# A recurrence's post-processing cut into six pieces, and the first interactions of each half recorded later

## The chip, the cores and the metric

The kernel runs on one core of one Trainium2 chip, with its five engines: TensorE (PE, matmuls), VectorE (DVE), ScalarE (ACT), GpSimd (POOL) and SyncE (SP, which issues DMAs). The metric is the device time of one execution in microseconds (us), lower is better. Each engine works off its own list of instructions in order; semaphores tie the lists together.

## The reference

An encoder trunk of two layers over 1024 tokens of width 1024, in fp32. Layer 0 mixes by a gated MLP and pooling, layer 1 by RWKV-7; a SwiGLU feed-forward network follows each, and a final RMS norm. The part that matters here is layer 1's mixer:

```python
def step(state, inp):                       # per token, 16 heads of 64
    r_t, w_t, k_t, v_t, a_t, b_t = inp
    sa = jnp.einsum('bhvk,bhk->bhv', state, a_t)
    state = (state * w_t[:, :, None, :] + sa[..., None] * b_t[:, :, None, :]
             + v_t[..., None] * k_t[:, :, None, :])
    return state, jnp.einsum('bhvk,bhk->bhv', state, r_t)
...
mean = jnp.mean(y, axis=-1, keepdims=True)
var = jnp.mean(jnp.square(y - mean), axis=-1, keepdims=True)
y = ((y - mean) * lax.rsqrt(var + GN_EPS)).reshape(bsz, seq, d)
y = y * ln_w.astype(f32) + ln_b.astype(f32)
bonus = jnp.sum(rh * kh * r_k.astype(f32), axis=-1, keepdims=True) * vh
y = (y + bonus.reshape(bsz, seq, d)).astype(h.dtype)
return (y * g) @ w_o, v_first
```

The state passes from token to token; the lines behind it, a norm over each head, its weight and bias, a bonus and a gate, are the post-processing that the change moves.

## The kernel before

The 1024 tokens are worked in two halves of 512, h = 0 and 1. A dense product in fp32 is three matmuls of split operands (high by high, low by high, high by low: lines 405 to 407); a weight tile of 512 KB is loaded by ACT's DMA queue into one of three raw buffers (`raw`), converted to its high part by ACT (L157: `whi`, `wdhi`) and to its low part by DVE (L158: `wlo`, `wdlo`).

The recurrence of a half (`recur`) goes through eight chunks, c = 0 to 7, of 64 tokens, 16 heads at a time. It runs beside the dense products of a feed-forward network: `drive` records both, step by step, at a ratio of 6.2 (half 0) or 3.0 (half 1), the steps of the recurrence with a higher priority. The number that a step yields says how much dense work is recorded before the next. The framework's scheduler then fixes each engine's list from these priorities and its own model of time; the kernel has no list of its own for this stretch.

The names of a chunk's work, in its order:

- `load(c)`: SP's DMAs of the chunk's operands (`ar`, `bk`, `uv`, `xx`).
- `gram(c, q)`, q = 0, 1: "first interactions", 32 matmuls `sm<-ar,bk` into two PSUM buffers, masked on DVE into `gt` (L1530).
- `flip_bk`: eight transposes `sm<-ident,bk` into two PSUM buffers, copied by ACT (L1541).
- `below`, `below2`: the inverse of the chunk's triangular part; `below2` ends with two copies into `XT` (ACT L1570, DVE L1571).
- `own`: `sm<-uv,gt` and `sm<-S,ar`, joined in `Q` (ACT L1582, DVE L1583).
- `ou`/`yp`: `sm<-Q,XT` and `yp<-S,ar`; `ou` is copied into `uv` (ACT L1605, DVE L1606).
- the state: `sm<-uv,bkt`, then two DVE operations (L1616, L1617) into the next `S`.
- `yp<-uv,gt` completes the output, copied into `ysb` (ACT L1629).

`burst(c)` records these for chunk c, with gram(c+1, 0) between own and ou, gram(c+1, 1) between ou and the state, and then flip_bk(c+1), load(c+2) and below(c+1). In this stretch PSUM has 3 buffers for dense products (`mm`), 4 for the recurrence (`sm`, used in turn) and one for `yp`.

After each odd chunk, `post` normalises the outputs of two chunks: DMAs of `gch` and `vch`, the bonus on POOL (L1668), 16 `bn_stats` on DVE (L1672), six small DVE operations for mean and variance (L1676 to L1681), the power −1/2 on POOL (`rsqrt`, L410), the mean's factor (L1683), the second chunk scaled on ACT (L1687, eight instructions), the first on DVE (L1690, L1691), and for each of the two a multiplication by the weight and the addition of `vch` (L1694, L1695). It is recorded as a whole between that chunk's burst and the next one's, in the middle of the dense work there, with three yields of 0.3. Then `turn_out`, called inside the next burst behind flip_bk, transposes the result on PE (`sm<-ident,ysb`, eight), gates it (L1711, eight on DVE) and stores it to `y_d`, from which the output projection reads it back.

Of the kernel before, what the change touches and what calls it, by code (L numbers as in the profile page):

```python
# [32 lines left out]
BESIDE = 2  # L33

# [9 lines left out]
def tile_trunk(  # L44
# [358 lines left out]

    def mm3(o, whi, wlo, xhi, xlo, first, last):
        pe.matmul(o, whi, xhi, start=first, stop=False)  # L405
        pe.matmul(o, whi, xlo, start=False, stop=False)  # L406
        pe.matmul(o, wlo, xhi, start=False, stop=last)  # L407
# [1053 lines left out]
    def recur(h, wp, stream):  # L1461
# [56 lines left out]
        def gram(c, q):  # L1518
            ar, bk, _, gt, _, _ = C[c]
            og = [pst("sm").rearrange("p (a b) -> p a b", b=P) for _ in range(2)]  # L1520
            for j in range(4):
                p = q * 4 + j
                for b in range(2):
                    for r in (1, 0):
                        mm(
                            og[r][rows[b], j, :], bk[rows[r], p, b, :],
                            ar[rows[r], p].rearrange("p a b -> p (a b)"), start=True, stop=True,
                        )
            for r in range(2):
                dve.tensor_tensor(  # L1530
                    out=gt[:, q * 4 : q * 4 + 4, r, :], in0=og[r], in1=bc(gm.unsqueeze(1), [P, 4, P]), op=ALU.mult
                )
# [27 lines left out]
        def below2(c, w1):  # L1560
            XT = C[c][5]
            ox = smt()
            for p in range(8):
                for r in (1, 0):
                    b0 = r * 64
                    mm(
                        ox[b0 : b0 + 32, p, 0:32], w1[b0 + 32 : b0 + 64, p, :], XT[b0 + 32 : b0 + 64, p, 32:64],
                        start=True, stop=True, tile_position=(b0 + 32, b0),
                    )
            act.activation(XT[0:32, :, 32:64], ox[0:32, :, 0:32], AF.Copy)  # L1570
            dve.tensor_copy(XT[64:96, :, 32:64], ox[64:96, :, 0:32])  # L1571

        def own(c, S0):
# [9 lines left out]
            dve.tensor_tensor(out=Q, in0=Q, in1=oq, op=ALU.add)  # L1583
            return Q

        def burst(c, bkt, w1):
# [3 lines left out]
            below2(c, w1)  # L1590
            Q = own(c, S0)
            yield 0.1
            if more:
                gram(c + 1, 0)
                yield 0.1
# [10 lines left out]
            dve.tensor_copy(uv[rows[1], 1], ou[rows[1]])  # L1606
            yield 0.1
            if more:
                gram(c + 1, 1)
                yield 0.1  # L1610
            if cg < NCH - 1:
# [5 lines left out]
                dve.tensor_tensor(out=Sn, in0=tS, in1=bc(pct[:, cg, :].unsqueeze(2), [P, 8, 64]), op=ALU.mult)  # L1617
                S[0] = Sn
                if c == 7:
# [13 lines left out]
            if more:  # L1633
                bkt = flip_bk(c + 1)
                if turned:
                    turned.pop()()
# [15 lines left out]
        turned = []  # L1652

        def post(jj):
# [14 lines left out]
            st = wt("st", 1, [P, 2, 8, 6])  # L1669
            for r in range(2):  # L1670
                for p in range(8):
                    dve.bn_stats(out=st[:, r, p, :], in_=ysb[r][:, p, :])  # L1672
            sts = st.rearrange("p a b s -> p (a b) s")
# [8 lines left out]
            rsqrt(var)  # L1682
            dve.scalar_tensor_tensor(out=mean, in0=mean, scalar=-0.5, in1=var, op0=ALU.mult, op1=ALU.mult)  # L1683
            yield 0.3
# [7 lines left out]
            yield 0.3  # L1692
# [3 lines left out]
            yield 0.3  # L1696
# [28 lines left out]
        yield 0.2  # L1725
# [7 lines left out]
        for c in range(8):  # L1733
            bkt, w1 = yield from burst(c, bkt, w1)
            yield BURST / 2
            if c % 2 == 1:
                yield from post(c // 2)
            yield BURST / 2
        turned.pop()()
# [225 lines left out]
    drive(ffn(0, 1, nxt["hn"], f, D0P[:3], nd=2), recur(0, wp, in_pieces(hb_pool, 1, h_d[1, 0])), 6.2)  # L1965
# [67 lines left out]
    drive(until(dense_a, flag), recur(1, wp, in_pieces(hp, 0, h_d[0, 1])), RATIO)  # L2033
# [44 lines left out]
```

## Time and profile before

| | us |
|---|---|
| median of three runs | 2395.51 |
| lowest, highest run | 2394.72, 2399.97 |
| the profiled execution | 2406.34 |
| its span | 2404.6 |
| PE busy in the span | 2324.9 |
| half 0's recurrence, about | 1042 to 1243 |
| half 1's recurrence, about | 1593 to 1810 |

The profile is one execution. A row of a timeline gives the start and the duration in us, the engine, the line of the kernel, what is written and read, and in brackets how long the engine had been idle and which operation released it. A row of waits gives the total, the number and the longest of such idle times. A row of windows gives a stretch and its length, each engine's busy time and instructions, and at its end PE's granted clock (1.00 is full), the DMA engines' busy share and GB/s.

### The profile page before, as it was taken

Reading aid. Unit: us, or ns where it says so; the run is one execution under the profiler, and the core shown is the slowest. Engines: PE = TensorE matmul, PEld = TensorE weight load, DVE = VectorE, ACT = ScalarE, POOL = GpSimd, SP = SyncE. Lnnn points to the kernel's source line nnn. Section 1 sums busy time; section 2 is a strip of 40 time slices with the busy share of each in tenths; the row PEclk is TensorE's granted clock in tenths of the full one; section 3 lists DMA queues with packets and bytes.
Section 4 is the critical chain, followed back from the end, with each engine's and each line's share of the span. In section 5 each row is a group of like instructions: output and inputs, shape, how many; then the busy total and the mean of one; then the engine's idle time right before and its main releaser. Section 6 shows DMA issues by size and latency. Waiting matters only on the chain.

```text
span 2404.6 us, 37640 instructions
## 1 busy us (share of the span) xinstructions
PE 2324.9 (97%) x15315; PEld 1903.6 (79%) x15315; DVE 1468.1 (61%) x2312; ACT 946.1 (39%) x1427; POOL 180.0 (7%) x226
## 2 busy tenths in 40 slices
PE   8999999999999999989999899999999999999998
PEld 6888888888788788777877678777778788888886
DVE  6445775665568858756768858756654446444443
ACT  6233444343224755423336555433332225222223
POOL 0200000000000022101100122101100001000001
PEclk9999999999999999999999999999999999999999
DMA  5114452334765565774545465676524333433231
GB/s 181 53 51 145 148 165 86 125 98 151 279 224 191 164 165 140 218 208 138 145 140 150 156 179 150 198 216 175 145 80 152 120 87 118 127 96 97 79 114 45
DMA packets 408333, 342.73 MB, mean 143 GB/s; under 512 B 79392, under 2 KB 352928, under 8 KB 407392
## 3 DMA queue, kind: packets, MB, share of 16 engines
q10 hardware_dynamic: 266048, 195.33, 27.4%
q1 hardware_dynamic: 142112, 145.01, 19.4%
q8 instruction: 120, 1.97, 0.3%
q14 instruction: 53, 0.43, 0.1%
HBM read 263.33 MB, written 76.94 MB: 142 GB/s over the span
## 4 chain that ended last, share of the span: by engine, by line
PE 75%; DVE 9%; DMA 7%; ACT 3%; issue 3%; POOL 2%; SPq 1%; ACTq 0%; POOLq 0%; DVEq 0%
PE mm L405 17%; PE mm L406 16%; PE mm L407 16%; PE mm L736 5%; PE mm L738 5%; PE mm L737 5%; PE sm L1483 4%; DVE wlo L158 1%; DMA raw<-in_ffn_w_down_dram 1%; DVE it L1435 1%; ACT whi L157 1%; DMA bk<-bk_d 1%; DVE xi L1440 1%; DMA raw<-y_d 1%; PE yp L1483 1%
## 5 line engine op out<-in xcount | busy, mean ns | idle before, releaser
L405 PE MATMUL mm<-ahi,whi 128*128 128x512 f32 x1376 | 541.7, 395 | 6.9 <-ACT ahi L157 4.9
L406 PE MATMUL mm<-alo,whi 128*128 128x512 f32 x1376 | 542.0, 394 | 3.0 <-DVE alo L158 3.0
L407 PE MATMUL mm<-ahi,wlo 128*128 128x512 f32 x1376 | 540.9, 394 | 1.0 <-DVE wlo L158 0.9
L157 ACT ACTIVATE whi<-raw 128x1024 fp32r<-128x1024 f32 (+2 forms) x284 | 286.1, 1014 | 491.8 <-PE mm L406 383.4
L158 DVE TENSOR_TENSOR wlo<-raw,whi 128x1024 fp32r<-128x1024 f32 (+2 forms) x284 | 337.4, 1192 | 220.4 <-ACT whi L157 193.6
L405 PEld LDWEIGHTS mm<-ahi,whi 128*128 128x128 f32 x1376 | 259.2, 188 | 65.3 <-ACT ahi L157 6.1
L406 PEld LDWEIGHTS mm<-alo,whi 128*128 128x128 f32 x1376 | 259.6, 189 | 60.4 <-DVE alo L158 4.3
L407 PEld LDWEIGHTS mm<-ahi,wlo 128*128 128x128 f32 x1376 | 259.5, 189 | 58.4 <-DVE wlo L158 2.3
L499 DVE TENSOR_TENSOR h<-h,mm 128x512 f32<-128x512 f32 x276 | 186.1, 684 | 160.2 <-PE mm L407 149.0
L405 PE MATMUL mm<-hidhi,wdhi 128*128 128x512 f32 x304 | 117.9, 394 | 2.8 <-ACT sg L953 2.8
L407 PE MATMUL mm<-hidhi,wdlo 128*128 128x512 f32 x304 | 119.0, 392 | 0.0
L406 PE MATMUL mm<-hidlo,wdhi 128*128 128x512 f32 x304 | 118.9, 392 | 0.0
L736 PE MATMUL mm<-ahi,whi 128*128 128x512 f32 x296 | 115.6, 390 | 0.0
L737 PE MATMUL mm<-alo,whi 128*128 128x512 f32 x296 | 115.2, 389 | 0.0
L738 PE MATMUL mm<-ahi,wlo 128*128 128x512 f32 x296 | 113.6, 389 | 0.0
L157 ACT ACTIVATE wdhi<-raw 128x1024 fp32r<-128x1024 f32 x42 | 43.5, 1057 | 166.7 <-PE mm L406 122.2
L961 DVE TENSOR_TENSOR sg<-sg,mm 128x512 f32<-128x512 f32 x52 | 35.7, 686 | 116.6 <-PE mm L407 116.6
L158 DVE TENSOR_TENSOR wdlo<-raw,wdhi 128x1024 fp32r<-128x1024 f32 x42 | 53.2, 1266 | 28.9 <-ACT wdhi L157 28.9
L405 PEld LDWEIGHTS mm<-hidhi,wdhi 128*128 128x128 f32 x304 | 57.5, 189 | 15.4 <-ACT sg L953 3.2
L407 PEld LDWEIGHTS mm<-hidhi,wdlo 128*128 128x128 f32 x304 | 57.4, 189 | 12.3 <-issue 0.3
L406 PEld LDWEIGHTS mm<-hidlo,wdhi 128*128 128x128 f32 x304 | 57.5, 189 | 11.8 <-issue 0.2
L405 PE MATMUL mm<-xhi,whi 128*128 128x512 f32 (+1 forms) x160 | 65.4, 409 | 0.0
(394 smaller groups left out, 4243.4 us busy)
## 6 DMA issues: line engine op xcount, KB each, us to landing
raw<-in_ffn_w_down_dram ACTq DMA_DIRECT2D x88, 512.0 KB
raw<-in_ffn_w_gate_dram ACTq DMA_DIRECT2D x74, 512.0 KB
raw<-in_ffn_w_up_dram ACTq DMA_DIRECT2D x74, 512.0 KB
hid_d<-hid SPq DMA_DIRECT2D x36, 512.0 KB
hd<-hid_d SPq DMA_DIRECT2D x26, 512.0 KB
raw<-in_ab_w_in_dram ACTq DMA_DIRECT2D x16, 512.0 KB
raw<-in_ab_w_out_dram ACTq DMA_DIRECT2D x16, 512.0 KB
raw<-in_rwkv_w_r_dram ACTq DMA_DIRECT2D x16, 512.0 KB
```

The source lines that it names most:

```text
L157: act.activation(hi, src, AF.Copy)
L158: (eng or dve).tensor_tensor(out=lo, in0=src, in1=hi.bitcast(F32), op=ALU.subtract)
L405: pe.matmul(o, whi, xhi, start=first, stop=False)
L406: pe.matmul(o, whi, xlo, start=False, stop=False)
L407: pe.matmul(o, wlo, xhi, start=False, stop=last)
L499: dve.tensor_tensor(out=H[h][:, m, :], in0=H[h][:, m, :], in1=o, op=ALU.add)
L736: pe.matmul(o, wh[:, k, :], x[0][:, k, :], start=st, stop=False, skip_group_check=True)
L737: pe.matmul(o, wh[:, k, :], x[1][:, k, :], start=False, stop=False, skip_group_check=True)
L738: pe.matmul(o, wl[:, k, :], x[0][:, k, :], start=False, stop=k == 3, skip_group_check=True)
L961: dve.tensor_tensor(out=s, in0=s, in1=o, op=ALU.mult)
L1435: dve.tensor_tensor(out=t, in0=bc(iat[:, j, j + 1 : 32].unsqueeze(2), sh), in1=bc(xi[:, j, 0 : j + 1].unsqueeze(1), sh), op=ALU.mult,)
L1483: i = f(*args, **kw)
```

## The change

`post` becomes a generator of six pieces and is no longer recorded in one go between two bursts. Its first step (the DMAs and the bonus) is taken after the odd chunk as before. The pieces are taken inside the next chunk's burst by `between()`, each recorded so that it stands behind the last DVE instruction of the chain step before it (`chain[0]`): the first chunk's bn_stats behind XT, the second's behind Q, mean to power behind gt, the scaling behind uv, and the two weight-and-`vch` pairs behind the second gt and the state. So the bn_stats of the even chunk, which stood behind that chunk's own burst, now stand two bursts later with the rest. After chunk 7 the remaining pieces are recorded with yields of 0.3.

`START` is the other edit: the first gram of a half is recorded behind two more dense products, and its first matmul is ordered behind the newest dense matmul.

```diff
--- before.py
+++ after.py
@@ -31,6 +31,8 @@
 BESIDE = 2
+
+START = 2
 
@@ -401,10 +403,12 @@
     def hsl(h):
         return slice(h * HT, (h + 1) * HT)
 
+    newest = [None]
+
     def mm3(o, whi, wlo, xhi, xlo, first, last):
         pe.matmul(o, whi, xhi, start=first, stop=False)
         pe.matmul(o, whi, xlo, start=False, stop=False)
-        pe.matmul(o, wlo, xhi, start=False, stop=last)
+        newest[0] = pe.matmul(o, wlo, xhi, start=False, stop=last).ins
 
     def rsqrt(t):
         pool.tensor_tensor(out=t, in0=t, in1=mhalf[:, : t.shape[1]], op=ALU.pow)
@@ -1458,7 +1462,7 @@
             )
     state_d = dram.tile([P, 8, 64], F32, name="state_d")
 
-    def recur(h, wp, stream):
+    def recur(h, wp, stream, ratio):
 
 
 
@@ -1527,9 +1531,9 @@
                             ar[rows[r], p].rearrange("p a b -> p (a b)"), start=True, stop=True,
                         )
             for r in range(2):
-                dve.tensor_tensor(
+                chain[0] = dve.tensor_tensor(
                     out=gt[:, q * 4 : q * 4 + 4, r, :], in0=og[r], in1=bc(gm.unsqueeze(1), [P, 4, P]), op=ALU.mult
-                )
+                ).ins
 
         def flip_bk(c):
             bk = C[c][1]
@@ -1568,7 +1572,7 @@
                         start=True, stop=True, tile_position=(b0 + 32, b0),
                     )
             act.activation(XT[0:32, :, 32:64], ox[0:32, :, 0:32], AF.Copy)
-            dve.tensor_copy(XT[64:96, :, 32:64], ox[64:96, :, 0:32])
+            chain[0] = dve.tensor_copy(XT[64:96, :, 32:64], ox[64:96, :, 0:32]).ins
 
         def own(c, S0):
 
@@ -1580,7 +1584,7 @@
                     mm(oq[rows[r], p, :], ar[rows[r], p, 0, :], S0[rows[r], p, :], start=True, stop=True)
             Q = wt("Q", 1, [P, 8, 64])
             act.activation(Q, ov, AF.Copy)
-            dve.tensor_tensor(out=Q, in0=Q, in1=oq, op=ALU.add)
+            chain[0] = dve.tensor_tensor(out=Q, in0=Q, in1=oq, op=ALU.add).ins
             return Q
 
         def burst(c, bkt, w1):
@@ -1588,10 +1592,13 @@
             ar, _, uv, gt, _, XT = C[c]
             cg, S0, more = h * 8 + c, S[0], c < 7
             below2(c, w1)
+            between()
             Q = own(c, S0)
+            between()
             yield 0.1
             if more:
                 gram(c + 1, 0)
+                between()
                 yield 0.1
             ou = smt()
             yp = psum["pool"].tile([P, 8, 64], F32, tag="y", bufs=1, name="yp")
@@ -1603,10 +1610,12 @@
                         skip_group_check=True,
                     )
             act.activation(uv[rows[0], 0], ou[rows[0]], AF.Copy)
-            dve.tensor_copy(uv[rows[1], 1], ou[rows[1]])
+            chain[0] = dve.tensor_copy(uv[rows[1], 1], ou[rows[1]]).ins
+            between()
             yield 0.1
             if more:
                 gram(c + 1, 1)
+                between()
                 yield 0.1
             if cg < NCH - 1:
                 Sn = wt("S", 2, [P, 8, 64])
@@ -1614,8 +1623,10 @@
                 each(os_, lambda r, p: bkt[:, p, r * 64 : r * 64 + 64], lambda r, p: uv[:, r, p, :])
                 tS = wt("Q", 1, [P, 8, 64])
                 dve.tensor_tensor(out=tS, in0=S0, in1=os_, op=ALU.add)
-                dve.tensor_tensor(out=Sn, in0=tS, in1=bc(pct[:, cg, :].unsqueeze(2), [P, 8, 64]), op=ALU.mult)
+                chain[0] = dve.tensor_tensor(out=Sn, in0=tS, in1=bc(pct[:, cg, :].unsqueeze(2), [P, 8, 64]), op=ALU.mult)
+                chain[0] = chain[0].ins
                 S[0] = Sn
+                between()
                 if c == 7:
                     sp.dma_start(state_d, Sn)
                 yield 0.1
@@ -1632,7 +1643,9 @@
             yield 0.1
             if more:
                 bkt = flip_bk(c + 1)
-                if turned:
+                if turned or pieces:
+                    for _ in pieces.pop():
+                        pass
                     turned.pop()()
                 if c < 6:
                     load(c + 2)
@@ -1649,7 +1662,12 @@
                 yield 0.1
             return bkt, w1
 
-        turned = []
+        turned, chain, pieces = [], [None], []
+
+        def between():
+            if pieces:
+                with tc.issue_after(chain[0]):
+                    next(pieces[0], None)
 
         def post(jj):
             ysb = [ypair.pop(0) for _ in range(2)]
@@ -1667,9 +1685,11 @@
             b16 = bon[:, 2 * j : 2 * j + 2, :].rearrange("t c p -> t (c p)")
             pool.tensor_tensor(out=v16, in0=v16, in1=bc(b16.unsqueeze(2), [P, 16, 64]), op=ALU.mult)
             st = wt("st", 1, [P, 2, 8, 6])
+            yield
             for r in range(2):
                 for p in range(8):
                     dve.bn_stats(out=st[:, r, p, :], in_=ysb[r][:, p, :])
+                yield
             sts = st.rearrange("p a b s -> p (a b) s")
             mean, dm, var = (wt(n, 1, [P, 16]) for n in ("mean", "dm", "var"))
             me, mo, ve, vo = (sts[:, :, i] for i in (1, 4, 2, 5))
@@ -1680,8 +1700,8 @@
             dve.tensor_tensor(out=var, in0=var, in1=dm, op=ALU.add)
             dve.tensor_scalar(out=var, in0=var, scalar1=1.0 / 64, scalar2=GN_EPS, op0=ALU.mult, op1=ALU.add)
             rsqrt(var)
+            yield
             dve.scalar_tensor_tensor(out=mean, in0=mean, scalar=-0.5, in1=var, op0=ALU.mult, op1=ALU.mult)
-            yield 0.3
             vb, mb = (bc(t[:, 0:8].unsqueeze(2), [P, 8, 64]) for t in (var, mean))
             for p in range(8):
                 act.activation(
@@ -1689,11 +1709,12 @@
                 )
             dve.tensor_tensor(out=ysb[0], in0=ysb[0], in1=vb, op=ALU.mult)
             dve.tensor_tensor(out=ysb[0], in0=ysb[0], in1=mb, op=ALU.add)
-            yield 0.3
+            yield
             for q in range(2):
                 dve.tensor_tensor(out=ysb[q], in0=ysb[q], in1=lnw, op=ALU.mult)
                 dve.tensor_tensor(out=ysb[q], in0=ysb[q], in1=vch[:, q], op=ALU.add)
-            yield 0.3
+                if q == 0:
+                    yield
 
             def turn_out():
                 for q in range(2):
@@ -1722,7 +1743,8 @@
             stream_loaded = stream()
         with tc.issue_after(stream_loaded):
             load(1)
-        yield 0.2
+        yield START * ratio
+        last.append(newest[0])
         gram(0, 0)
         yield 0.5
         gram(0, 1)
@@ -1734,8 +1756,11 @@
             bkt, w1 = yield from burst(c, bkt, w1)
             yield BURST / 2
             if c % 2 == 1:
-                yield from post(c // 2)
+                pieces[:] = [post(c // 2)]
+                next(pieces[0])
             yield BURST / 2
+        for _ in pieces[0]:
+            yield 0.3
         turned.pop()()
         yield 1.0
 
@@ -1962,7 +1987,7 @@
     between = []
     prime_b, steps_b = down_steps(1, D0B[1], lambda f: whl(), hslot, True, spill_h, (next(between[0]) for _ in range(4)))
     prime_b()
-    drive(ffn(0, 1, nxt["hn"], f, D0P[:3], nd=2), recur(0, wp, in_pieces(hb_pool, 1, h_d[1, 0])), 6.2)
+    drive(ffn(0, 1, nxt["hn"], f, D0P[:3], nd=2), recur(0, wp, in_pieces(hb_pool, 1, h_d[1, 0]), 6.2), 6.2)
     wp_es.close()
     y, y_es = open_pool(name="y0", bufs=1, side="left")
     ys = open_act(("y", 0), y)
@@ -2030,7 +2055,7 @@
         1, 0, hnA, f, TAIL, last=True, between=y_pieces(), early=True,
         then={G1A[1][-1][-1]: lambda: flag.append(1), G1A[2][0][-1]: out_b},
     )
-    drive(until(dense_a, flag), recur(1, wp, in_pieces(hp, 0, h_d[0, 1])), RATIO)
+    drive(until(dense_a, flag), recur(1, wp, in_pieces(hp, 0, h_d[0, 1]), RATIO), RATIO)
     wp_es.close()
     ps_es.close()
     ps_es = open_psum("psd2", DENSE)
```

What this does to the lists, at the places that the prediction speaks of. (In the new kernel the same operations have line numbers that are 2 to 21 higher.)

DVE, half 0, the burst of chunk 4, before: from the copy into XT to the masks of gram(5, 1).

```order
L1571 COPY XT<-sm 32x8x32
L1690 TENSOR_TENSOR ysb<-ysb,var 128x512
L1683 SCALAR_TENSOR_TENSOR mean<-mean,var 128x16
L1691 TENSOR_TENSOR ysb<-ysb,mean 128x512
L1583 TENSOR_TENSOR Q<-Q,sm 128x512
L1694 TENSOR_TENSOR ysb<-ysb,lnw 128x512
L1695 TENSOR_TENSOR ysb<-ysb,vch 128x512
L1694 TENSOR_TENSOR ysb<-ysb,lnw 128x512
L1695 TENSOR_TENSOR ysb<-ysb,vch 128x512
L1530 TENSOR_TENSOR gt<-sm,gm 128x4x128 x2
L1606 COPY uv<-sm 64x512
L1530 TENSOR_TENSOR gt<-sm,gm 128x4x128 x2
```

The same place after, in two parts, first from XT to the second gt of gram(5, 0):

```order
L1575 COPY XT<-sm 32x8x32
L1691 BN_STATS st<-ysb 128x6 x8
L1587 TENSOR_TENSOR Q<-Q,sm 128x512
L1691 BN_STATS st<-ysb 128x6 x8
L1534 TENSOR_TENSOR gt<-sm,gm 128x4x128
L1696 TENSOR_TENSOR mean<-st 128x16
L1534 TENSOR_TENSOR gt<-sm,gm 128x4x128
```

and from the last small operation ahead of the power to the state's two operations:

```order
L1701 TENSOR_SCALAR var<-var 128x16
L1613 COPY uv<-sm 64x512
L1704 SCALAR_TENSOR_TENSOR mean<-mean,var 128x16
L1710 TENSOR_TENSOR ysb<-ysb,var 128x512
L1711 TENSOR_TENSOR ysb<-ysb,mean 128x512
L1534 TENSOR_TENSOR gt<-sm,gm 128x4x128
L1714 TENSOR_TENSOR ysb<-ysb,lnw 128x512
L1534 TENSOR_TENSOR gt<-sm,gm 128x4x128
L1715 TENSOR_TENSOR ysb<-ysb,vch 128x512
L1625 TENSOR_TENSOR Q<-S,sm 128x512
L1626 TENSOR_TENSOR S<-Q,pct 128x512
```

The 16 bn_stats and the small rows now stand between XT and uv, and the mean row, which takes the power's result from POOL, with two wide `ysb` rows stands between uv and the second pair of gt.

PE, the same burst, from gram(5, 1) on. Before:

```order
L1483 MATMUL sm<-ar,bk 64x128 x16
L1483 MATMUL sm<-uv,bkt 64x64 x16
L1483 MATMUL yp<-uv,gt 64x64 x16
L1483 MATMUL sm<-ident,bk 128x128 x8
L1483 MATMUL sm<-ident,ysb 128x128 x8
L405 MATMUL mm<-ahi,whi 128x512
L406 MATMUL mm<-alo,whi 128x512
```

After:

```order
L1487 MATMUL sm<-ar,bk 64x128 x16
L1487 MATMUL sm<-uv,bkt 64x64 x16
L1487 MATMUL yp<-uv,gt 64x64 x16
L1487 MATMUL sm<-ident,bk 128x128 x8
L1487 MATMUL sm<-ident,ysb 128x128
L410 MATMUL mm<-alo,whi 128x512
L411 MATMUL mm<-ahi,wlo 128x512
```

The first transpose of `ysb` still follows the flips directly; the other seven stand behind 11 dense matmuls. Further up in the same burst (rows not shown), 18 dense matmuls stood inside gram(5, 0) before; now 4 stand between gram(5, 0) and ou.

PE, half 0, the first gram, before:

```order
L405 MATMUL mm<-hidhi,whi 128x512
L406 MATMUL mm<-hidlo,whi 128x512
L407 MATMUL mm<-hidhi,wlo 128x512
L406 MATMUL mm<-hidlo,whi 128x512
L407 MATMUL mm<-hidhi,wlo 128x512
L1485 MATMUL sm<-ar,bk 64x128
L1483 MATMUL sm<-ar,bk 64x128 x31
L405 MATMUL mm<-hidhi,whi 128x512
```

After:

```order
L409 MATMUL mm<-hidhi,whi 128x512
L410 MATMUL mm<-hidlo,whi 128x512
L411 MATMUL mm<-hidhi,wlo 128x512
L410 MATMUL mm<-hidlo,whi 128x512
L411 MATMUL mm<-hidhi,wlo 128x512
L1487 MATMUL sm<-ar,bk 64x128 x32
L409 MATMUL mm<-hidhi,whi 128x512
L410 MATMUL mm<-hidlo,whi 128x512
```

The same dense matmuls stand ahead of the first gram; in half 1 it stands two dense matmuls later. Only the line through which its first matmul is issued differs.

## The prediction, made before the changed kernel had run

> **What bounds the kernel now.** I read the page's busy times first, then PE's waits in the two stretches where the recurrence runs beside the dense products (1020 to 1260 and 1580 to 1830 us), then the timeline rows of those waits, then DVE, ACT and POOL there. Waits print as total, times, longest.
>
> ```profile
> PE 2324.9 (97%) x15315; PEld 1903.6 (79%) x15315; DVE 1468.1 (61%) x2312; ACT 946.1 (39%) x1427; POOL 180.0 (7%) x226
> PE sm L1483 <- DVE gt L1530: 3.6, 2, 2.7
> PE sm L1485 <- DMA bk<-bk_d: 3.5, 1, 3.5
> PE mm L405 <- ACT ahi L157: 3.3, 1, 3.3
> PE sm L1483 <- DVE XT L1571: 2.4, 1, 2.4
> ...
> PE sm L1483 <- DVE gt L1530: 7.7, 2, 6.9
> PE sm L1485 <- DMA bk<-bk_d: 5.9, 1, 5.9
> ```
>
> PE is busy for 2324.9 of the 2404.6 us span. No matmul is added or removed, so only the other 79.7 us and the clock can move. The rows on gt and XT say that PE stands still when a small operation of the chain comes late on DVE. Of these, the following lie in the bursts of chunks 2, 4 and 6, the bursts that the change loads with post-processing:
>
> ```profile
> 1102.28 1.10 PE L1483 MATMUL sm<-ar,bk 64*64 64x128 f32 x30 [2.36 <-DVE XT L1571]
> 1148.76 1.10 PE L1483 MATMUL sm<-ar,bk 64*64 64x128 f32 x30 [0.88 <-DVE gt L1530]
> 1149.78 1.38 PE L1483 MATMUL sm<-uv,bkt 128*64 128x64 f32 x31
> 1151.06 1.10 PE L1483 MATMUL yp<-uv,gt 128*64 128x64 f32 x31
> 1152.09 1.09 PE L1483 MATMUL sm<-ident,bk 128*128 128x128 f32 x8
> 1153.02 1.04 PE L1483 MATMUL sm<-ident,ysb 128*128 128x128 f32 x8
> 1656.03 1.10 PE L1483 MATMUL sm<-ar,bk 64*64 64x128 f32 x30 [1.11 <-ACT Q L1582]
> 1659.39 1.10 PE L1483 MATMUL sm<-ar,bk 64*64 64x128 f32 x30 [0.86 <-DVE gt L1530]
> 1749.30 1.98 PE L1483 MATMUL sm<-ar,bk 64*64 64x128 f32 x30 [6.86 <-DVE gt L1530]
> ```
>
> These six bursts lose 2.36 + 0.88 + 1.97 + 6.86 = 12.1 us now (the two pieces of 1.11 and 0.86 belong to one burst; two bursts lose next to nothing). The starts also price PE's steps: gram 1.0, uv·bkt 1.3, yp·gt 1.0, eight flips 0.9 us. Own, ou/yp are 1.0 each: own runs from 1098.55 to 1099.54.
>
> ```profile
> 1098.55 0.27 PE L1483 MATMUL sm<-uv,gt 64*64 64x64 f32 x1
> 1099.54 0.38 PE L1483 MATMUL sm<-ar,bk 64*64 64x128 f32 x2
> 1093.26 0.40 PE L406 MATMUL mm<-alo,whi 128*128 128x512 f32 x1
> 1093.49 0.40 PE L407 MATMUL mm<-ahi,wlo 128*128 128x512 f32 x1
> ```
>
> A dense matmul advances PE by 0.23 us (the last two starts).
>
> **The prices of the pieces.**
>
> ```profile
> 1092.03 1.11 DVE L1672 BATCH_NORM_STATS2 st<-ysb 128x6 f32<-128x64 f32 x8 [0.46 <-ACT ysb L1629]
> 1093.17 0.18 DVE L1676 TENSOR_TENSOR mean<-st 128x16 f32<-128x16 f32 x1
> 1094.12 0.43 DVE L1557 COPY w<-sm 32x256 f32<-32x256 f32 x1
> 1097.20 0.69 DVE L1690 TENSOR_TENSOR ysb<-ysb,var 128x512 f32<-128x512 f32 x1 [2.65 <-POOL var L410]
> 1101.80 0.42 DVE L1571 COPY XT<-sm 32x256 f32<-32x256 f32 x1
> 1102.98 0.69 DVE L1583 TENSOR_TENSOR Q<-Q,sm 128x512 f32<-128x512 f32 x1
> 1103.58 0.68 DVE L1530 TENSOR_TENSOR gt<-sm,gm 128x512 f32<-128x512 f32 x1
> L410 POOL TENSOR_TENSOR var<-var,small x8: 2899/2905/3907, 1094.2 to 1786.3; 128x16 f32<-128x16 f32 x8
> ```
>
> Eight bn_stats cost DVE 1.11 us, the six small rows 0.95 (1093.17 to 1094.12), each of the six wide ysb operations about 0.69, and the power on POOL 2.9. Now the bn_stats of the earlier chunk and the wait for POOL (2.65 us of idle DVE, 1094.55 to 1097.20) fall into the dense stretch ahead of the burst, where PE needs nothing from DVE. After the change both stand inside the burst.
>
> **The sum, burst by burst.** I walk half 0's chunk 4, whose new order is shown ahead of this: 4 dense matmuls between gram and ou, none between gram' (of q = 1) and uv·bkt. Time 0 is the end of ox, where XT's copy and PE's own start. DVE: XT 0.4, bn_stats 1.5, Q 2.35 (ACT's half of it ends at 1.6), bn_stats 3.45, gt 4.1 and 4.85, the small rows 5.7, uv 6.4. POOL runs from 5.75 to 8.65, then DVE: mean 8.85, two ysb operations 10.2, gt' 10.85, one more ysb 11.55, gt' 12.2, the vch addition 12.9. PE: own to 1.0, gram 2.0, 4 dense 2.95, ou 3.95. PSUM's four sm buffers go round, so gram' needs the buffer that the first gt frees: a stall of 0.25. uv·bkt waits from 5.2 to 6.4 for uv: 1.2. It and yp·gt end at 8.7; the second half of the flips (at 9.2) needs the buffer that the first gt' frees at 10.85: 1.65. The first ysb transpose, at 11.3, waits for the vch addition at 12.9: 1.6. Together **4.7 us** in place of 0.9. Before, 18 dense matmuls (4.1 us) stood inside that burst's gram and hid post-processing.
>
> By the same walk: half 0's chunk 2 has 9 and then 2 + 6 dense matmuls there, which hide gt, uv and nearly the whole flip wait, and leaves 1.75; chunk 6, and half 1's chunk 4, with 2 and none, 5.15 each. Half 1's chunk 2 has the copies of two weight tiles ahead of XT on ACT: XT is late by about 1.4, Q by 1.5, gt by 1.1, gt' by 0.5, 4.5 in all. In half 1's chunk 6 the long stall stays:
>
> ```profile
> 1738.18 0.35 ACTq L121 DMA_DIRECT2D raw<-in_ffn_w_down_dram  x1
> 1744.49 1.06 ACT L157 ACTIVATE wdhi<-raw 128x1024 fp32r<-128x1024 f32 x1 [7.02 <-DMA raw<-in_ffn_w_down_dram]
> 1745.58 1.93 DVE L158 TENSOR_TENSOR wdlo<-raw,wdhi 128x1024 fp32r<-128x1024 f32 x1 [5.66 <-ACT wdhi L157]
> ```
>
> A weight load is issued at 1738.18, its conversion waits 6.3 us for it, and gt queues on DVE behind wdlo. In the new order the same load, conversion and wdlo still stand ahead of gt (and, on ACT, of uv), at the same dense product; 13 fewer dense matmuls (3.0 us) lie between, one other wlo (1.2) leaves the queue ahead of gt, and the late ysb adds 1.0: between 7 and 10.3, I take 9.
>
> Sum 1.75 + 4.7 + 5.15 + 4.5 + 5.15 + 9 = 30.2, less 12.1: **+18.1 us**. From below: if only uv's 1.2 and half of the flip and ysb waits stay (2.8 a burst, 7 for the last), 21 and +9. From above, every burst 1.0 worse (POOL's longest power, 3.907 in place of 2.905, which all that is queued behind it follows): +24.1.
>
> **The end of half 0.** Here the change gives something back.
>
> ```profile
> 1243.23 0.53 SPq L1714 DMA_DIRECT2D y_d<-gch  x1
> 1246.83 1.67 ACTq L121 DMA_DIRECT2D raw<-y_d  x3
> 1253.17 1.06 ACT L157 ACTIVATE ahi<-raw 128x1024 fp32r<-128x1024 f32 x1 [2.55 <-DMA raw<-y_d]
> 1254.28 0.64 PE L405 MATMUL mm<-ahi,whi 128*128 128x512 f32 x1 [3.33 <-ACT ahi L157]
> 1250.00:1260.00 10.00, 6.05 (x17) 4.13 (x16) 7.14 (x9) 4.83 (x6) 0.20 (x1) 0.72 0.96 322
> ```
>
> The last y goes out at 1243.23 and comes back converted at 1254.2; PE has 45 dense matmuls (10.2 us) behind the last transposes and then stands for 3.33, at a clock of 0.72 in that window. The recurrence takes fewer dense matmuls into its bursts after the change, so 92 (20.9 us) remain there. The 3.33 goes, and with it some 2 us of slow clock (about 6 us of work at 0.72). But on ACT the first y conversion then stands ahead of a later weight's, and pieces 2 to 4 of y wait for the three raw buffers, which can cost 0 to 3. I take −5 in all, bounds −8 and 0.
>
> **The first interactions.** Both halves begin with a stall for bk (3.5 and 5.9). In the new order the first gram has the same dense product ahead of it in half 0, and two matmuls (0.46) more in half 1. So I give it −0.5, bounds −2 and 0. SP's moved vch loads are needed first by the vch additions, over ten microseconds behind: nothing. POOL's memsets likewise.
>
> **The clock.**
>
> ```profile
> 1100.00:1110.00 10.00, 7.72 (x145) 5.80 (x145) 7.30 (x13) 3.25 (x7) 2.06 (x2) 1.00 0.49 134
> 1740.00:1750.00 10.00, 3.15 (x64) 2.36 (x60) 4.42 (x5) 3.11 (x4) 1.90 (x1) 0.80 0.43 124
> 1750.00:1760.00 10.00, 10.00 (x149) 8.68 (x146) 6.97 (x22) 1.86 (x4) 0.00 (x0) 0.86 0.34 101
> ```
>
> The third number from the end is the granted clock. 2.36 us of stall left it at 1.00; 6.86 took it to 0.80 and then 0.86, and the gram behind took 1.98 in place of 1.10. The new stalls come in pieces of at most 1.65, so I charge nothing; if the pieces of a burst counted together, gram, uv·bkt and the rest would lose some 2 us in each of the three tight bursts, 6 in all. [...]
>
> **Total:** +18.1 − 5 − 0.5 = +12.6. My walk lets no step start before its queue does, but prices each handover at its full length; I take 2 off for that: +10.5. Against the profiled execution of 2406.34 (span 2404.6) that is 2416.8; against the median of the runs, 10.8 lower at 2395.51, **2406 us**.
>
> **Rivals.** A measurement of this kernel can tell about 0.2%, 4.8 us, from no change.
>
> *It comes out even.* The bursts cost only their lower bound of +9 and the end of half 0 pays its full 8: +0.5, or 2396. For it: the tight bursts differ by a dense matmul or two from ones that lose nothing now. Against: DVE's rows above fill 12.9 us of a burst in which PE has 8.1 us of work up to the flips' end.
>
> *Faster.* The place is DVE's queue ahead of XT and gt. Now L1691, L1694 and L1695 stand ahead of XT in half 0's chunk 2 (2.36 us) and wlo ahead of gt in half 1's chunk 6; with each piece behind a chain step, the 2.36 goes, the 6.86 shrinks by up to 3, and POOL's 2.9 is covered if ou, gram' and uv·bkt take that long. It decides from the point where gt' runs before PE's second flips, that is if mean is released 1.65 us earlier than I have it. Then each burst keeps about 1.2, the last 4.5: 10.5, −1.6; with −8 at the end of half 0, −9.6: 2386. Were START to hide the bk stalls as well, another −9. Against it: the mean row stands ahead of gt' in every one of the six.
>
> *Slower still.* The stalls of a burst add up for the clock (+6), or a weight conversion behind y's costs its 3: 2414.
>
> *It doesn't do what it says:* START moves the first grams by nothing or two matmuls; that is in the sum already.
>
> **Chances.** The forecast 0.50, even 0.20, faster 0.20, slower still 0.10. The forecast's own range is 2400 to 2412; with the others cut at one in ten on each side, 2388 to 2415. Faster by over 0.2%: 0.22; within: 0.25; slower: 0.53.
>
> **What would show it.** In the trace after: PE waits on uv (L1613 and L1612) of about 1.2 in three bursts; stalls in the flips for gt (1.65) and on the first lone ysb transpose (1.6); DVE idle on POOL's var in each burst for some 2 us; no 3.33 stall on ahi; both bk stalls still there; the 6 to 7 us stall in half 1's chunk 6. I am wrong if PE's waits in the six bursts sum to less than 20 us, or if the clock falls below 0.95 in a burst with no stall over 2.5 us.

## The result

The changed kernel is slower. Its four runs go from 2415.57 to 2423.48 us (median 2419.71), those of the kernel before beside them from 2394.72 to 2404.83 (median 2397.74). The ratio on record is 1.0068, 95% interval 1.005 to 1.0086, which is 16 us (12 to 21); the medians lie 22 us apart. Timed again with other runs beside it (last experiment below) the ratio was 1.0077, interval 1.0054 to 1.0099. The forecast was +10.5 us: the direction is right, the size two thirds of the 16 us and half of the 22.

The profile after, in the views that were read before. First the page's busy times, then PE's waits in the bursts of half 0 (1095 to 1225 us) and of half 1 (1640 to 1830 us), printed as total, times, longest.

```profile
PE 2334.2 (96%) x15315; PEld 1911.1 (79%) x15315; DVE 1468.0 (61%) x2312; ACT 945.2 (39%) x1427; POOL 177.9 (7%) x226
PE sm L1487 <- DVE gt L1534: 3.8, 2, 1.9
PE sm L1487 <- DVE ysb L1715: 3.7, 3, 1.2
...
PE sm L1487 <- DVE gt L1534: 5.1, 2, 3.2
PE sm L1487 <- DVE ysb L1715: 2.7, 3, 1.1
PE sm L1487 <- DVE Q L1587: 1.6, 2, 1.4
PE sm L1487 <- DVE XT L1575: 1.4, 1, 1.4
```

The profiled execution has a span of 2421.8 us, 17.2 more than the one before. PE's idle time in it is 87.6 us, 7.9 more; the other 9.3 us is PE being busy longer (2334.2 against 2324.9) with the same 15315 matmuls. So in this execution one half of the loss is waiting and the other half is slower work. That split is not a fixed one: in a second execution of the changed kernel (last experiment) PE was idle for 12.3 us more than before and busy for 2.7 us more.

The waiting stands where the walk had put it. PE in half 0's chunk 4, chunk 6, and half 1's chunks 2, 4 and 6:

```profile
1146.60 0.57 PE L1487 MATMUL sm<-uv,bkt 128*64 128x64 f32 x12 [0.29 <-DVE uv L1613]
1151.19 0.66 PE L1487 MATMUL sm<-ident,bk 128*128 128x128 f32 x4 [1.92 <-DVE gt L1534]
1153.07 0.45 PE L1487 MATMUL sm<-ident,ysb 128*128 128x128 f32 x1 [1.23 <-DVE ysb L1715]
1173.37 0.23 PE L1487 MATMUL sm<-Q,XT 64*64 64x64 f32 x1 [2.00 <-issue]
1195.58 0.66 PE L1487 MATMUL sm<-ident,bk 128*128 128x128 f32 x4 [1.92 <-DVE gt L1534]
1659.59 1.10 PE L1487 MATMUL sm<-ar,bk 64*64 64x128 f32 x30 [1.42 <-DVE XT L1575]
1662.14 0.33 PE L1487 MATMUL sm<-Q,XT 64*64 64x64 f32 x1 [1.45 <-DVE Q L1587]
1715.82 0.84 PE L1487 MATMUL sm<-ident,bk 128*128 128x128 f32 x4 [1.92 <-DVE gt L1534]
1760.32 1.83 PE L1487 MATMUL sm<-ar,bk 64*64 64x128 f32 x30 [3.20 <-DVE gt L1534]
```

Three flip waits of 1.92 and the waits on the lone ysb transpose are new. DVE's rows of chunk 4 show what they wait for:

```profile
1145.85 0.69 DVE L1613 COPY uv<-sm 64x512 f32<-64x512 f32 x1
1148.90 0.18 DVE L1704 SCALAR_TENSOR_TENSOR mean<-mean,var 128x16 f32<-128x16 f32 x1 [2.36 <-POOL var L414]
1149.71 0.69 DVE L1711 TENSOR_TENSOR ysb<-ysb,mean 128x512 f32<-128x512 f32 x1
1150.44 0.69 DVE L1534 TENSOR_TENSOR gt<-sm,gm 128x512 f32<-128x512 f32 x1
1152.24 0.68 DVE L1715 TENSOR_TENSOR ysb<-ysb,vch 128x512 f32<-128x512 f32 x1
```

DVE stands for 2.36 us on POOL's power, then does two ysb operations (L1710, L1711), and only then the gt that frees the flips' buffer. PE's 1151.19 follows that gt; its 1153.07 follows the vch addition.

The slower work is the clock. Windows of 10 us in chunk 4, in chunk 5 (with the 2.00 us wait), in chunk 6 and in half 1's chunks 2, 4 and 6; the granted clock is the third number from the end:

```profile
1150.00:1160.00 10.00, 7.58 (x60) 6.07 (x61) 8.53 (x16) 5.28 (x12) 0.00 (x0) 0.83 0.33 106
1170.00:1180.00 10.00, 8.00 (x204) 6.89 (x202) 4.62 (x8) 2.15 (x4) 0.61 (x2) 0.83 0.44 116
1190.00:1200.00 10.00, 6.07 (x79) 4.94 (x80) 7.44 (x15) 4.20 (x11) 2.90 (x1) 0.87 0.01 2
1200.00:1210.00 10.00, 10.00 (x164) 8.14 (x163) 8.02 (x25) 1.35 (x3) 1.91 (x1) 0.96 0.41 111
1660.00:1670.00 10.00, 8.55 (x195) 7.12 (x187) 8.14 (x30) 2.39 (x7) 3.54 (x3) 0.83 0.52 139
1710.00:1720.00 10.00, 6.38 (x88) 5.00 (x81) 7.41 (x15) 4.20 (x11) 3.51 (x3) 0.81 0.35 98
1720.00:1730.00 10.00, 10.00 (x71) 8.05 (x70) 5.30 (x13) 1.92 (x3) 1.61 (x1) 0.85 0.80 195
1757.00:1767.00 10.00, 6.80 (x103) 5.09 (x101) 6.08 (x15) 3.68 (x9) 2.90 (x1) 0.83 0.19 54
```

Ten times what is missing to 1.00, summed over these rows, is 12 us of lost clock, at the most, since PE also stands in part of that time. Before, in the same bursts, only half 1's chunk 6 lost any, 3.4 by its two windows that the prediction shows (0.80 and 0.86). These amounts vary from one execution to the next: the second execution of the changed kernel lost 8.5 us there, and the kernel with START alone, whose PE list is that of before in these bursts, lost 6.8.

The end of half 0 gave back what was expected. The 3.33 us wait on ahi is gone; the longest left is for h:

```profile
1262.87 0.50 PE L409 MATMUL mm<-hd,whi 128*128 128x512 f32 x1 [1.35 <-DVE h L503]
1250.00:1260.00 10.00, 9.00 (x38) 6.68 (x37) 8.31 (x10) 5.11 (x7) 0.00 (x0) 1.00 0.53 158
```

Before, this window stood at 0.72, as the prediction shows, and the next one at 0.93:

```profile
1260.00:1270.00 10.00, 9.47 (x40) 7.00 (x39) 6.48 (x10) 3.18 (x3) 1.01 (x1) 0.93 0.68 165
```

### The profile page after: what moved, and what is told of

Same layout as the page of the kernel before. It is cut to its first block, busy times and chain, and to the rows that moved or that the text cites. A ratio compares the mean times of both kernels' runs of the same rounds, so it can differ in the third digit from the quotient of the medians.

```text
span 2421.8 us, 37652 instructions
## 1 busy us (share of the span) xinstructions
PE 2334.2 (96%) x15315; PEld 1911.1 (79%) x15315; DVE 1468.0 (61%) x2312; ACT 945.2 (39%) x1427; POOL 177.9 (7%) x226
## 4 chain that ended last, share of the span: by engine, by line
PE 76%; DVE 9%; DMA 7%; ACT 3%; issue 3%; POOL 2%; SPq 1%; ACTq 0%; POOLq 0%; DVEq 0%
PE mm L409 17%; PE mm L411 17%; PE mm L410 17%; PE mm L740 5%; PE mm L742 5%; PE mm L741 5%; PE sm L1487 3%; DVE wlo L160 1%; DMA raw<-y_d 1%; ACT whi L159 1%; DMA bk<-bk_d 1%; POOL var L414 1%; PE aux L1411 1%; PE aux L1412 1%; PE mm L590 1%
## 5 line engine op out<-in xcount | busy, mean ns | idle before, releaser
L410 PEld LDWEIGHTS mm<-hidlo,wdhi 128*128 128x128 f32 x304 | 57.5, 189 | 12.1 <-issue 0.5
```

## The experiments

Each kernel is compared with runs of the kernel before on the same chip; a ratio over 1 is slower than before. The diffs are against the changed kernel unless said otherwise.

### START alone

```diff
 (against the kernel before)
-        yield 0.2
+        yield START * ratio
+        last.append(newest[0])
         gram(0, 0)
```

> The kernel before with the START edit alone: first gram recorded behind two more dense products and ordered behind the newest dense matmul, post-processing as before. My reading: the order of PE's list stays as before, bk still comes late, so the time is that of the kernel before within 0.2% (ratio 0.998 to 1.002) and both bk stalls stay (3 to 6 us together with the gt stall in half 0, about 6 in half 1). Rival, START carries the loss: ratio 1.004 or more. Rival, START hides bk: ratio 0.996 or less, bk stalls under 1 us.

Measured: ratio 0.9996, interval 0.9978 to 1.0015. START does nothing that can be measured, which leaves it up to 5 us either way. Both kinds of start stalls are still there in half 0:

```profile
1035.31 3.57 PE L1487 MATMUL sm<-ar,bk 64*64 64x128 f32 x64 [2.35 <-DMA bk<-bk_d]
1042.00 0.85 PE L1487 MATMUL sm<-ident,bk 128*128 128x128 f32 x4 [2.19 <-DVE gt L1534]
```

In half 1 the two were 1.6 and 1.5, less than the 6 expected, but over all kernels of this study, with and without START, the first wait for bk varies between 0.8 and 5.9 us, so one execution says nothing of it.

### The pieces alone

```diff
-        yield START * ratio
-        last.append(newest[0])
+        yield 0.2
         gram(0, 0)
```

> The changed kernel without the START edit (first grams as before, six pieces kept). My reading: the pieces carry the whole loss, so ratio 1.005 to 1.009, with the same waits in the bursts of chunks 2, 4 and 6: three waits of 1.9 us in the flips for gt, 0.8 to 1.2 on the lone ysb transpose in every one of the six bursts, about 20 us together. Rival, START carries it: ratio 1.002 or less.

Measured: ratio 1.0053, interval 1.0036 to 1.007, with flip waits of 1.92, 1.92 and 1.93 and ysb waits of 0.84 to 1.56. The pieces carry the loss; the interval overlaps with that of both edits together (1.005 to 1.0086).

### The power left out

```diff
-            rsqrt(var)
             yield
             dve.scalar_tensor_tensor(out=mean, in0=mean, scalar=-0.5, in1=var, op0=ALU.mult, op1=ALU.mult)
```

> The changed kernel with the power -1/2 on POOL left out of the group norm (the output is scaled by the variance instead of its inverse root), so that the mean row on DVE waits for nothing. My theory, that DVE standing on POOL's 2.9 us with gt' queued behind it makes the flip waits: the three flip waits of 1.9 us go, the ysb waits of 1.2 fall to under 1, PE's waits in the six bursts fall from 20.6 us to 12 to 14, and with the shorter stalls two or three of the half-clock periods behind the bursts go as well (1.7 us each): 8 to 12 us less than the changed kernel, ratio 1.002 to 1.004. Rival, the sheer amount of DVE work in the burst does it, not POOL: the flip waits shrink by less than 0.7 us each, ratio 1.005 to 1.008. Rival, the clock periods come by chance and not from the stalls: their number behind the bursts stays though the stalls go.

Measured: ratio 1.0003, interval 0.9985 to 1.0022. PE's waits in half 0's bursts (1095 to 1225) and the windows of chunks 4 and 6:

```profile
PE sm L1487 <- DVE ysb L1714: 2.1, 2, 1.0
...
1150.00:1160.00 10.00, 10.00 (x77) 8.20 (x76) 7.24 (x16) 3.73 (x5) 0.00 (x0) 1.00 0.68 172
1190.00:1200.00 10.00, 10.00 (x164) 8.26 (x165) 8.75 (x25) 1.75 (x4) 1.91 (x1) 1.00 0.45 119
```

No flip wait is left anywhere, the ysb waits are 1.0, and the windows that stood at 0.83 and 0.87 stand at 1.00. The waits of all bursts come to 10 us, below the 12 to 14 expected, and the ratio is below the 1.002 to 1.004 expected. In half 0's bursts PE's list is that of the changed kernel, but for one pair of neighbours, so there the waits go with the power alone. For half 1 the scheduler made another list, where the ysb waits are gone too and one gt behind a weight conversion waits 2.9; what the power alone does there is not separated. Without POOL's 2.9 us in DVE's way the loss is gone, to within the 5 us that the interval leaves. That half 0's clock recovers with the stalls speaks against periods that come by chance.

### The scaling one step later

```diff
             chain[0] = dve.tensor_copy(uv[rows[1], 1], ou[rows[1]]).ins
-            between()
             yield 0.1
```

> The changed kernel with each piece from the scaling on taken one chain step later (none behind uv; scaling behind the second gt, the weight pairs behind the state), so that gt' no longer queues behind the mean row. My theory: the flip waits of 1.9 us go, but the lone ysb transpose, still right behind the flips, waits for a vch addition that is no earlier: its 1.2 us grow to about 3, so that PE's waits in the bursts stay at 18 to 22 us and the ratio at 1.005 to 1.009. Rival, the order of gt' and mean alone is the cause: waits in the bursts 13 or less, ratio 1.004 or less.

Measured: ratio 0.9999, interval 0.9982 to 1.0017. The expectation was wrong, and both conditions of its rival were met (waits of 13 or less, a ratio of 1.004 or less): the ysb waits did not grow, they went. The waits of the bursts are 1.3 us in half 0 and 5.1 in half 1, 6.4 against 20.6. But the order of gt' and mean was not all that changed. In PE's list of half 0 the scheduler now put 26 to 44 dense matmuls (6 to 10 us) between the flips and the transposes of ysb, which stand together again. But the transposes are ordered ahead of below, so the whole chain moved back with them, and half 0's last transposes came 86 dense matmuls later, with 6 behind them ahead of the output projection (92 in the changed kernel). So a loss turned up at the end of half 0, from 1225 to 1310:

```profile
PE aux L444 <- DVE nacc L423: 5.5, 1, 5.5
PE mm L409 <- ACT whi L159: 4.2, 2, 2.3
PE mm L409 <- ACT ahi L159: 3.3, 1, 3.3
```

With two smaller ones (1.7 and 0.9) that is 15.6 us of waits; before it was 7.0, in the changed kernel 4.6. So this run can't tell how much the order of gt' and mean is worth by itself.

### The transposes in the next odd chunk's burst

```diff
             if more:
                 bkt = flip_bk(c + 1)
-                if turned or pieces:
+                if pieces:
                     for _ in pieces.pop():
                         pass
-                    turned.pop()()
...
                 yield 0.1
+            if c % 2 and turned:
+                turned.pop()()
             for p in range(8):
```

> The changed kernel with the transposes of the finished pair (and the gate and store behind them) taken in the next odd chunk's burst, behind its state, instead of right behind the flips of the even chunk's burst. My theory: the six ysb waits (0.8 to 1.2 us) go since ysb was ready long before, the flip waits stay where little dense work stands between gram' and uv·bkt, and are hidden where 2 + 5 matmuls stand there; the end of half 0 stays as cheap as in the changed kernel (under 5 us of waits from 1225 to 1310), since the last transposes keep their place: waits in all bursts under 12 us, ratio 0.996 to 1.002. Rival, the gate's eight DVE operations, now in the odd burst, make XT, Q or gt late there: as much as before comes back, ratio over 1.004.

Measured: ratio 1.0028, interval 1.0014 to 1.0042, between the two ranges that were expected. The ysb waits are gone, and in half 0 the flip waits too; the gate's work on DVE there makes w late by 1.2 and 1.7. In half 1's bursts (1640 to 1830) gt waits stay, and as much is lost on issue, in waits that no operation ends (more on them at the end):

```profile
PE sm L1487 <- DVE w L1561: 2.9, 2, 1.7
...
PE sm L1487 <- issue: 4.5, 2, 3.3
PE sm L1487 <- DVE gt L1534: 4.4, 4, 1.9
```

### Both moves

The two diffs above together.

> Both moves: the scaling behind the second gt (none behind uv), and the finished pair's transposes in the next odd chunk's burst. My theory: flip and ysb waits both go, waits in the bursts 8 us or less (half 1's chunk 2 and 6 keep what their weight conversions cost), fewer half-clock periods, and no long wait at the end of half 0: 12 to 18 us less than the changed kernel and less than before, ratio 0.993 to 0.998. Rival, the waits move once more (end of half 0, as in the kernel with the scaling alone moved, 15 us there): ratio 0.999 to 1.003.

Measured: ratio 1.0087, interval 1.0065 to 1.011, the highest of all ratios (its interval overlaps with the changed kernel's), and a miss for the theory and for its rival. The waits on gt and ysb are gone as expected and the end of half 0 costs 5.7. What came is a wait that no operation releases:

```profile
1157.76 1.56 PE L1487 MATMUL sm<-ar,bk 64*64 64x128 f32 x24 [3.79 <-issue]
1710.12 1.30 PE L1487 MATMUL sm<-ar,bk 64*64 64x128 f32 x17 [5.33 <-issue]
```

These 9.1 us stand where gram follows own directly. They cover about half of the 21 us by which this kernel's runs exceed those before. The rest is open: the profiled execution itself was only 10.6 us over the one before.

### The transposes behind below

```diff
 (with the scaling one step later, as above)
                     for _ in pieces.pop():
                         pass
-                    turned.pop()()
...
                 w1 = below(c + 1)
                 yield 0.1
+                if turned:
+                    yield 1.5
+                    turned.pop()()
             return bkt, w1
```

> The changed kernel with the scaling behind the second gt, and the transposes of the pair recorded behind below of the same burst. In PE's list they stand behind below with no dense matmul ahead in half 0's chunk 4, but the half's last ones stay ahead of all products from spilled hidden values, as in the changed kernel. My theory: the flip waits go, a ysb wait of 2 to 3 us remains in those bursts where no dense matmul stands between, none at the end of half 0: ratio 0.998 to 1.003. Rival, the end of half 0 loses its 15 us whatever is done to the bursts: ratio 1.004 or more.

Measured: ratio 1.0027, interval 1.0014 to 1.004. PE's waits in half 0's bursts:

```profile
PE sm L1487 <- DVE ysb L1716: 5.2, 3, 3.9
```

The flip waits of the tight bursts are gone; the transposes, with no dense matmul ahead, wait 3.86 for ysb in half 0's chunk 4 and 3.85 in half 1's chunk 6 (2 to 3 were expected). The end of half 0 costs 5.3, near the changed kernel's 4.6. So the long waits at the end of half 0, in the kernel with the scaling alone, came with the place of the last transposes. In time their going bought nothing: the ratio is 1.0027 here and was 0.9999 there, and what makes up the difference stays open.

### A mixture by half, and the changed kernel once more

Half 0 with the transposes in the next odd burst, half 1 with the scaling one step later.

```diff
             chain[0] = dve.tensor_copy(uv[rows[1], 1], ou[rows[1]]).ins
-            between()
+            if h == 0:
+                between()
...
-                    turned.pop()()
+                    if h:
+                        turned.pop()()
...
+            if h == 0 and c % 2 and turned:
+                turned.pop()()
```

> By half: half 0 as in the kernel with the pair's transposes in the next odd burst (its half 0 took 2.8 us less than before from 1021 to 1371), half 1 as in the kernel with the scaling behind the second gt (its half 1 took 6.4 us less from 1548 to 1876). If the losses belong to the places where they were read, the two add up: 9 us less than before, ratio 0.994 to 0.999, waits in the bursts 12 us or less and under 6 us at the end of half 0. Rival, these differences are scatter between executions: ratio 0.999 to 1.003.

Measured: ratio 1.0009, interval 0.9999 to 1.002. Half 0 did as read (3.4 of waits in its bursts), half 1 did not: new waits for Q (1.9) and on issue (1.9) came in its bursts, and one for gt (3.5) ahead of them. The waits are within what was expected (under 10 in the bursts, 5.5 at the end of half 0), the time is not: the 9 us that the two single executions promised do not add up. This is the rival's range, scatter between executions, and no run excludes it. No kernel of this study measurably beats the one before.

> The changed kernel once more, beside the mixture on one chip. If the short stalls of the bursts and the half-clock periods that they set off belong to its order and not to one execution: the same waits to 0.1 us in the tight bursts (1.92 in the flips, 1.23 on the lone ysb transpose), half-clock periods again behind the bursts of chunks 4 and 6 in both halves, ratio 1.005 to 1.009. Rival, the periods come by chance: waits the same, periods at other places, ratio nearer 1.004.

Measured: ratio 1.0077, interval 1.0054 to 1.0099. In half 0 the flip waits (1.92) and the ysb waits (1.23) repeat to the hundredth, and the clock falls behind the same chunks. Chunk 4:

```profile
1150.38 0.66 PE L1487 MATMUL sm<-ident,bk 128*128 128x128 f32 x4 [1.92 <-DVE gt L1534]
1152.26 0.45 PE L1487 MATMUL sm<-ident,ysb 128*128 128x128 f32 x1 [1.23 <-DVE ysb L1715]
1150.00:1160.00 10.00, 8.39 (x65) 6.77 (x66) 8.78 (x19) 4.47 (x10) 0.00 (x0) 0.83 0.34 112
```

In half 1 the flip wait repeats too, but a ysb wait grew from 0.82 to 1.55, and the clock did not repeat. It stayed at 1.00 behind chunk 2, where it had been 0.83:

```profile
1660.00:1670.00 10.00, 8.19 (x182) 6.36 (x176) 8.11 (x27) 2.76 (x8) 3.54 (x3) 1.00 0.46 126
```

Behind chunk 4 it lost 1.7 us where it had lost 3.4. The loss belongs to this kernel's order, not to one execution; its part of clock varies.

## Why the prediction was right, and which terms were off

**The six bursts.** The walk named the right waits in the right places; it priced them too high. By burst, forecast and measured (from the profile after):

| burst | forecast | measured |
|---|---|---|
| half 0, chunk 2 | 1.75 | 1.23 |
| half 0, chunk 4 | 4.7 | 0.29 + 1.92 + 1.23 = 3.4 |
| half 0, chunk 6 | 5.15 | 0.27 + 0.20 + 0.78 + 1.92 + 1.23 = 4.4 |
| half 1, chunk 2 | 4.5 | 1.42 + 1.45 + 0.82 = 3.7 |
| half 1, chunk 4 | 5.15 | 0.19 + 0.65 + 1.92 + 1.05 = 3.8 |
| half 1, chunk 6 | 9 | 3.20 + 0.83 = 4.0 |
| sum | 30.2 | 20.6 |

Against the 12.1 of before that is +8.5 where +18.1 was forecast (+7.8 if three waits of under 0.3, which the 12.1 leaves out, are counted before as they are here). Two sizes were wrong. In the tight bursts every wide DVE operation was given its full 0.69; rows that wait for nothing start some 0.60 apart (1151.05, 1151.64, 1152.24 on DVE in chunk 4), and the pieces of uv's wait were 0.3 to 0.8 rather than 1.2. The 2 us taken off at the end for this were too few. And in half 1's chunk 6 the weight's conversion began 5.1 us after the load's issue, not 6.3, and at that issue PE had 11 dense matmuls ahead of gram, so that it came to its long wait later: 3.20, not over 6.

**The end of half 0.** Forecast −5. The waits fell from 7.0 (1225 to 1310) to 4.6, and the clock, at 0.72 and 0.93 in two windows before (3.5 us), stayed at 1.00: −5.9.

**START.** Forecast −0.5; alone it measured 0.9996, so nothing that can be measured.

**The clock.** This is the step that failed: "The new stalls come in pieces of at most 1.65, so I charge nothing". In the profile after, the charge was 12.0 − 3.4 = 8.6 us, as much as the new waits; 1.7 of it stands behind the wait on issue in chunk 5, which is not one of them. By the second execution (8.5) it was 5.1, and against START alone (6.8) 5.2 and 1.7. So the term is some 2 to 9 us, where nothing was charged. It was the rival "slower still", which was given 6 us and one chance in ten. Of the prediction's two signs of being wrong, one came true, a clock below 0.95 in a burst with no stall over 2.5 us; the other, waits of less than 20 us, was missed by 0.6.

That stalls of this size cost no clock was the author's estimate, and the trace after decides against it: in chunk 4 no gap is over 1.92 us and PE works between them; they sum to 3.44 us between 1146.3 and 1153.1, and the window from 1150 stands at 0.83, in both executions of this kernel (3.9 us in the second). With 0.27 and 1.04 left (the power left out) it stands at 1.00. Nor did the longest wait alone decide: 2.36 us left the clock at 1.00 before, 1.92 did not after. And before, behind a wait of 2.75 us that the prediction did not show, it stood at 0.50:

```profile
1049.18 0.68 PE L1483 MATMUL sm<-ident,bk 128*128 128x128 f32 x4 [2.75 <-DVE gt L1530]
1049.68:1053.09 3.41, 3.41 (x13) 2.74 (x12) 1.92 (x4) 1.19 (x2) 0.00 (x0) 0.50 1.13 293
```

**The sum.** +8.5 for waits, +8.6 for clock, −5.9 at the end of half 0: +11.2. With the 2.00 us wait on issue in chunk 5, which was not foreseen, and 0.56 more on issue in chunk 4, +13.8. The profiled executions differ by 17.2, so 3 to 4 us are not placed; waits before the recurrences scatter by that much from one execution to the next. (The second execution gives +9.4, +5.1, −6.2 and 2.3 on issue, +10.6 of its 15.0.) The forecast of +10.5 came near because an overpriced term of waits stood in for a clock term that was left out. The direction and the places were read; the size was luck.

**The mechanism**, DVE queued behind POOL with gt' behind it, is shown for half 0 by leaving the power out (no flip wait left in the same list of PE, ratio 1.0003 for the whole kernel); in half 1, whose list changed, it is argued. That the order of gt' and mean alone decides is not shown: with gt' ahead the ratio was 0.9999, but the scheduler answered each move with another list, and waits came up in other places.

## What to carry to other kernels

When slack work is queued behind steps of a critical chain on an in-order engine, follow the one row in it that waits for another engine: everything of the chain behind that row inherits the wait, here the 2.4 us of DVE on POOL. Short stalls of the matmul engine were not free for being short: in the traces before and after, half clock followed all 16 stretches of 3.41 us, counted as in the next section, of which PE had stood idle for more than 60%, some 2 us, in one stall or in several. Where these stretches begin was not known ahead of a run, so charge such stalls as a chance of slow clock; a half-clock period of 3.41 us costs up to 1.7 us (an estimate, half of its length). And where a scheduler makes the list, a moved step buys a new list: read where the dense work went, above all at the end of the stretch, before counting a gain.

## What was not expected of the hardware

**Stalls of one length went either way.** Nearly the same wait on XT left the clock at 1.00 in the execution before (2.36) and was followed by half clock in the kernel with START alone (2.38):

```profile
1093.47 0.92 PE L1487 MATMUL sm<-ar,bk 64*64 64x128 f32 x12 [2.38 <-DVE XT L1575]
```

In the traces before and after the granted clock is 1.00 or 0.50, and the 24 half-clock periods between 20 and 2370 us last 3.41 or 6.83 us; within each of the two traces all their starts and ends lie whole multiples of 3.413 us apart, to within 0.01 us. Laid out at such multiples, two stretches share the wait before; with START alone one that ends where the half clock begins took it whole. The rows are those two, then with START alone that one and the half-clock one behind it, then the same pair in chunk 4 of the changed kernel.

```profile
1097.46:1100.88 3.42, 2.46 (x101) 1.82 (x99) 3.35 (x6) 2.78 (x9) 0.00 (x0) 1.00 0.02 5
1100.88:1104.29 3.41, 2.01 (x34) 1.71 (x35) 3.32 (x7) 0.71 (x2) 0.00 (x0) 1.00 0.53 154
1090.11:1093.52 3.41, 1.03 (x62) 0.79 (x50) 3.31 (x6) 2.68 (x8) 0.00 (x0) 1.00 0.37 107
1093.52:1096.93 3.41, 3.41 (x34) 2.79 (x35) 2.59 (x4) 0.00 (x0) 0.00 (x0) 0.50 0.53 151
1149.55:1152.96 3.41, 0.66 (x4) 0.42 (x4) 3.34 (x7) 3.41 (x11) 0.04 (x1) 1.00 0.29 83
1152.96:1156.37 3.41, 3.30 (x9) 2.65 (x10) 2.55 (x4) 0.35 (x1) 0.00 (x0) 0.50 0.00 0
```

At full clock PE was busy for 2.46, 2.01, 1.03 and 0.66 us of a stretch, and only the last two of these were followed by half clock. Over the traces before and after, from 20 to 2370 us, 16 such stretches at full clock had PE busy for less than 40%, and all 16 were followed by half clock; of the 1304 with 70% or more, one was; between the two, 7 of 21. These are counts of two executions; what sets the clock is not shown.

**Some waits of PE are ended by no operation.** The waits "on issue" whose rows are shown above (2.00, 3.79 and 5.33 us) stand in runs of small matmuls with no dense ones between. The page after lists a queue that it calls "instruction":

```profile
q8 instruction: 120, 1.97, 0.3%
```

The traces before and after have three such waits of over 1 us: 3.24 us from 1082.7 before, 3.46 us from 1080.9 and 2.00 us from 1171.4 after. A packet of this queue starts 0.7 and 1.0 us after the first two begin and 0.4 us before the third, where packets come 3.5 to 14.6 us apart in half 0's bursts (after). For the 5.33 us wait, which began at 1704.8, none starts from 1697 to 1705 and one from 1705 to 1710. That this queue makes PE wait is not shown; no run changed it alone.
